# The end of the output projection: homes of the transposed parts, raw loads and the place of the last pair

## The chip, the cores and the metric

The kernel runs on one core of a Trainium2 chip. The metric is the device time of one execution in microseconds (us). The median of three runs of the kernel before is 1249.16 us (1244.13 to 1250.89).

PE is the matrix engine, DVE the vector engine, ACT the scalar engine, POOL the GpSimd engine, SP the engine that issues the DMAs. Each has its own queue of instructions and works through it in order; a semaphore holds the head of a queue back until what it needs is there.

## What is computed

One layer of an encoder block on 1024 tokens of width 1024, in float32:

```
u = RMSNorm(x);  [q|k|v|cB|cC|cH|gA|gB] = u @ W_in
A = neighbourhood attention(q, k, v, rpb);  B = cB * conv3(cC * cH)
m = sigmoid(gA) * (A @ W_A) + sigmoid(gB) * (B @ W_B)
x = x + m @ W_o
x = x + relu(RMSNorm(x) @ W1)^2 @ W2
```

The change lies where the product with `W_o` ends and the one with `W1` (1024 x 4096) begins.

## The kernel before

Every float32 operand of a matmul is split into two float16 parts, high and low, after scaling by a power of two, and each product takes three passes. The large products use a scheme with seven products in place of eight, so both operands are needed in seven forms (sums and differences of quarters).

**Order of the work.** The kernel is one long program, and what it issues on an engine is issued in the order in which its Python code runs. `unit` (L185) issues the matmuls of one unit and then calls `step()` and `tick()` some times. `step` advances all generators in the list `fg` by one `yield`; `tick` advances the first generator in `bg` that is not waiting. So the places of ACT's, DVE's and POOL's instructions among each other follow from the units at which the generators were advanced. `apart(mark, n, work)` lets a generator wait until `n` more matmul columns have been issued.

**Projection.** `proj(b, half)` computes one block of 128 tokens by 512 columns of `x + m @ W_o`; `tail(b, half, ...)` does so and then calls the given functions. The last eight blocks are the calls of `tail`, up to L1386. The actions are: `sq`, the sum of squares of a block for the norm (L1163); `begin` and `normal`, the scaling of a block into the form buffer `fv[0]` (L1173); `form_sums`, the additions that make seven forms of four quarters (L1155, DVE); `high(n, part)`, the float16 high part (L1189, ACT); `low(n, part)`, the low part (L1195, DVE) and the DMA that transposes both into `U2`, the moving operand of the next product (L1196, SP). Pairs `n` = 0 to 3 are 256 tokens each; part 0 are forms 0 to 3 (`u2T`), part 1 forms 4 to 6 (`u2x`). All pairs use the same float16 buffer `fv[1]`. `forms_m` makes the forms of weight group 1 (`mH` and others, L1293 to L1296); `g1` advances it. The last pair is done by `last_pair`, a generator in `fg` (L1391) that runs while PE is already in the next product.

**First MLP product.** `W1` is cut in 16 groups `q` of 256 columns. `quad(q)` issues seven units of 12 matmuls, in the order 1, 6, 5, 4, 2, 7, 3; what follows a unit is called its post:

| post | engine, line | |
|---|---|---|
| 1 | ACT L1453 | copy from PSUM |
| 6, 5 | DVE L1436, L1441 | need the copy |
| 2 | DVE L1455 | |
| 7 | DVE L1444, L1445, L1446 | three operations |
| 3 | DVE L1449 | then `h_done(q)` is put into `fg` |

`h_done(q)`: relu (L1410) and square (L1412) on ACT, four additions that make the forms of the next operand (`sums`, L1155), here on POOL, and the store to HBM (L1416). Quads 0 and 1 are done in two halves of 256 columns of the moving operand: the first halves of both, then the wait for pair 3, then the second halves. Their units take half as long, and the second halves go in the order 1, 2, 5, 4, 6, 7, 3.

**Weights of a group.** Each group has two raw pieces of 512 KB, loaded into five buffers `rawp` (L210). `load_upto` issues loads up to a count, less `held`, and not beyond `limit`. A group's preparation: `rows_scaled`, eight scalings of rows (L948, ACT); `forms_sum`, two sums of squares (L957, ACT) and four additions for the forms (L962, POOL); `sum_of`, a small reduction (L928) and a cast (L929) on DVE; `all_sum`, a matmul with ones that adds over the partitions (L179, PE), called the ones matmul below; the scale out of it (L182, L404 to L411, DVE); `forms_split`, four high parts (L977, ACT) and four low parts (L973, DVE). `sums1(q)` is the first half of this, `prep1(q)` the second, and `prep1(q)` goes on with `sums1(q + 1)`. Quad `q` needs group `q`; while quad `q` runs, the ones matmul of group `q + 2` and its split are issued.

The second MLP product follows at L1470 and below and is not touched.

Of the kernel before, what the change touches and what calls it, by code (L numbers as in the profile page):

```python
# [10 lines left out]
F32 = mybir.dt.float32  # L11
F16 = mybir.dt.float16
BF16 = mybir.dt.bfloat16
I32 = mybir.dt.int32
AF = mybir.ActivationFunctionType
OP = mybir.AluOpType
# [36 lines left out]
def encoder_block(ctx: ExitStack, tc: tile.TileContext, x, weights, cols, gqk, rel, masks, out):  # L53
    nc = tc.nc
    V, A, G, T, SP = nc.vector, nc.scalar, nc.gpsimd, nc.tensor, nc.sync

    base = ctx.enter_context(tc.tile_pool(name="base", bufs=1))
    rawp = ctx.enter_context(tc.tile_pool(name="rawp", bufs=5))
# [38 lines left out]
    def at(c, i, n=1):  # L97
        return slice(c.start + i, c.start + i + n)
# [18 lines left out]
    fg, bg = [], []  # L117
# [88 lines left out]
    loads, loaded, done, vhome, held, limit = [], [0], [0], [], [0], [10 ** 6]  # L206
# [5 lines left out]
    def load_upto(n):  # L212
        while loaded[0] < min(n - held[0], limit[0], len(loads)):
            ch, p = loads[loaded[0]]
            loaded[0] += 1
            t = rawp.tile([128, 1024], F32, name="raw")
            load_into(t[:, :ch.widths[p][0] * ch.widths[p][1]], ch, p)
            ch.raw.append(t)
# [103 lines left out]
    g1, g2, gm2 = at(consts, 0, 8), at(consts, 20, 8), keep()  # L322
    rows = {"A": lambda j: rowsA, "B": lambda j: rowsB, "O": lambda j: rowsM}
    chunks, offset = {}, 0
    for (kind, j), pieces in plan():
# [4 lines left out]
        for p, (k, w) in enumerate(ch.widths):  # L330
            ch.offs.append(offset)
            if kind != "X" and (kind, j) != ("1", 0) and (kind, j, p) != ("1", 1, 1):
# [3 lines left out]
    cV, cConv, cA, cB, cO, c1, c2, c2x = ([chunks[k, j] for j in range(n)] for k, n in  # L336
                                              (("V", 2), ("C", 4), ("A", 4), ("B", 4), ("O", 2),
                                               ("1", 16), ("2", 4), ("X", 4)))
# [120 lines left out]
    sq = w1p.tile([128, D], F32, name="sq", bufs=1)  # L459
# [84 lines left out]
    for p in range(11):  # L544
# [7 lines left out]
        for q in (p,) if p < 6 else (2 * p - 6, 2 * p - 5):  # L552
            c = q // 2 + 3
# [306 lines left out]
    for k in range(N + 11):  # L860
        p, w = k // 16, k % 16
# [212 lines left out]
    for n in range(8):  # L1074
# [19 lines left out]
        else:  # L1094
            push(cO[0])
            tick(4)
            y = w3p.tile([128, 4, 512], F32, name="gsum", bufs=1)
# [47 lines left out]
    U2 = (u2T,  # L1145
          w4p.tile([128, 3, 2, 4, 512], F16, name="u2x", bufs=1))
# [4 lines left out]
    def sums(f, sub):  # L1151

        z = [f[:, i] for i in range(7)]
        for o, a, b, op in ((5, 0, 2, OP.subtract), (2, 2, 3, OP.subtract), (4, 2, 0, OP.subtract), (6, 1, 4, OP.add)):
            sub.tensor_tensor(z[o], z[a], z[b], op=op)  # L1155
            yield

    pair_done, fv, ssq = [0], [], keep(10)
# [7 lines left out]
    def row_scale(col, n=1):  # L1166
        y = tmp(n)
        for _ in rstd(at(ssq, col, n), D, y, 9):
            pass
        return y  # L1170

    def normal(b, y):
        A.activation(fv[0][:, 2 * (b // 4):2 * (b // 4) + 2].rearrange("p a t -> p (a t)"), X1[:, b], AF.Copy,  # L1173
                     scale=sc[:, y])
# [9 lines left out]

    PART = ((0, 4), (4, 7))

    def high(n, part):
        a, b = PART[part]
        A.activation(fv[1][:, a:b, 0], fv[0][:, a:b], AF.Copy)  # L1189

    def low(n, part):

        f, v = fv
        a, b = PART[part]
        V.tensor_tensor(v[:, a:b, 1], f[:, a:b], v[:, a:b, 0], op=OP.subtract)  # L1195
        SP.dma_start_transpose(U2[a // 4][:, :, :, :, 128 * n:128 * n + 128]  # L1196
                               .rearrange("p f s k t -> p (f s k) t"), v[:, a:b].rearrange("p f s k -> p (f s k)"))
        pair_done[0] = n + part

    def form_sums():  # L1200
# [22 lines left out]
    def sums1(q):  # L1223

        ch = c1[q]
        if q == 2:
            yield from rows_scaled(ch, g2)
        if q == 0:
            tsum[0] = U2[1][:, 2].rearrange("p s k t -> p (s k t)").bitcast(F32).rearrange("p (i c) -> p i c", i=4)
        elif q % 2 == 0:  # L1230
            while q == 2 and pair_done[0] < 4:
                yield
            t = wsp.tile([128, 2, 4, 512], F32, name="tsum", tag="ws")
            for i in range(2):
                tsum[q + i] = t[:, i]
        if q != 2:
            yield from rows_scaled(ch, g2)
        yield from forms_sum(ch, tsum[q], 3 if q else 0)

    def prep1(q):  # L1240

        ch = c1[q]
        s, ch.inv = yield from scale_of(ch.sum, 9, 1)
        yield from gate(q)
        pool, tag = TAGS[q % 3]
        P = P1[q] = pool.tile([128, 7 if q else 8, 2, 512], F16, name="w16_1", tag=tag)
        yield from forms_split(ch, tsum[q], s, P)
        ready.add(q)
        if 1 < q < 15:
            yield from sums1(q + 1)  # L1250
# [1 line left out]
    SQJ = U2[1][:, 0, :, :, 384:512].rearrange("p s k t -> p (s k) t").bitcast(BF16)  # L1252
    scaled = []

    limit[0] = c1[3].first + 1

    def prep_m():

# [14 lines left out]
    def forms_m():  # L1273

        (w11, w12), (w21, w22) = ([c1[1].raw[i].rearrange("p (n m) -> p n m", n=2)[:, j] for j in range(2)]
                                  for i in range(2))
        s = scaled[0]
        two = rawp.tile([128, 1024], F32, name="raw").bitcast(F16).rearrange("p (f i c) -> p f i c", f=2, i=2)
        held[0], limit[0] = 1, 10 ** 6
        t2 = w4p.tile([128, 2, 512], F16, name="t2", bufs=1)  # L1280
        t4 = w4p.tile([128, 2, 512], F16, name="t4", bufs=1)
        k4 = lambda v: v.rearrange("p (k c) -> p k c", k=4)
        flat = {0: lambda i: P1[0][:, 7, i], 1: lambda i: two[:, 0, i], 2: lambda i: two[:, 1, i],
                5: lambda i: t2[:, i], 6: lambda i: t4[:, i]}

        def place(f, i):
            return k4(flat[f](i)) if f in flat else M[0][:, 4 * (f - 3):4 * (f - 3) + 4, 512 * i:512 * i + 128]

        P1[1] = lambda f, i, k: place(f, i)[:, k]
        src = {0: w11, 1: w21, 2: w22, 3: w11, 4: w12, 5: w22, 6: w21}  # L1290

        def hi(f):
            A.activation(place(f, 0), k4(src[f]), AF.Copy, scale=sc[:, s])  # L1293

        def lo(f):
            V.scalar_tensor_tensor(place(f, 1), k4(src[f]), sc[:, s], place(f, 0), op0=OP.mult, op1=OP.subtract)  # L1296

        def add(o, a, b):
            V.tensor_tensor(o, a, b, op=OP.add)

        hi(0), hi(2), hi(1), lo(0), add(w11, w11, w12), lo(2)
        yield
        add(w12, w12, w22)
        yield
        add(w22, w22, w11), lo(1), hi(5), add(w21, w21, w22), hi(6)
        yield
        lo(5), lo(6)
        yield
        hi(3), hi(4), lo(3)
        yield  # L1310
        lo(4)
        done[0] += 1
        load_upto(done[0] + 5)
        ready.add(1)

# [15 lines left out]
    def wait(n):  # L1331
        for _ in range(n):
            yield
# [7 lines left out]
    two = []  # L1341
# [9 lines left out]
    def tail(b, half, *acts):  # L1351
        proj(b, half, acts)
        for a in acts:
            a()
# [3 lines left out]
    def sq(b, half=None):  # L1358
        if half is None:
            return lambda: square(b, 2 * (b % 4) + b // 4)  # L1360
        return lambda: square(b, (6 if half == 0 else 8) + b // 4, slice(512 * half, 512 * half + 512))

    def row3(b):
        V.tensor_tensor(sc[:, at(ssq, 6 + b // 4)], sc[:, at(ssq, 6 + b // 4)], sc[:, at(ssq, 8 + b // 4)], op=OP.add)
        return row_scale(6 + b // 4)

    def do(f, *a):
        return lambda: f(*a)

    g1, tk = do(advance, chain), do(tick)  # L1370
# [6 lines left out]
    tail(5, 1, sq(1), form_sums, do(high, 0, 0), g1)  # L1377
    tail(2, 1, do(high, 0, 1), sq(5), do(low, 0, 0), do(begin, 1), do(low, 0, 1))
    tail(6, 1, sq(2), form_sums, do(high, 1, 0))
    tail(3, 0, sq(6), do(high, 1, 1), do(low, 1, 0), do(begin, 2), do(low, 1, 1))  # L1380
    tail(7, 0, sq(3, 0), form_sums, do(high, 2, 0), g1)
    bg.append(sums1(2))
    tail(3, 1, sq(7, 0), do(low, 2, 0), do(high, 2, 1), do(low, 2, 1), g1, tk)
    side[0] = False
    bg.extend(prep1(q) for q in range(2, 16))
    tail(7, 1, sq(3, 1), lambda: normal(3, row3(3)), tk)  # L1386
    fv[1] = wsp.tile([128, 7, 2, 512], F16, name="v16", tag="ws")

    def last_pair():
        sq(7, 1)()  # L1390
        y = row3(7)  # L1391
        yield from wait(3)
        normal(7, y)
        yield from wait(6)
        form_sums()
        high(3, 0), high(3, 1)
        yield from wait(6)
        low(3, 0), low(3, 1)

    fg.append(last_pair())  # L1400
    pe_done[0] = 0
# [6 lines left out]
    def h_done(q):  # L1408
        f = AS.pop(q)
        A.activation(f[:, 0:4], f[:, 0:4], AF.Relu)  # L1410
        yield
        A.activation(f[:, 0:4], f[:, 0:4], AF.Square, scale=sc[:, c1[q].inv],  # L1412
                     accum_out=sc[:, at(bsum[q // 4], q % 4)])
        yield
        yield from sums(f, G)
        SP.dma_start(HS[q // 4][:, :, q % 4], f)  # L1416
        live.remove(q)
        if q % 4 == 3:
            m = tmp()
            V.tensor_reduce(sc[:, m], sc[:, bsum[q // 4]], axis=AX, op=OP.max)  # L1420
            yield
            yield from pow2(m, 14, *R[q // 4])
            r_ready[q // 4] = True
# [293 lines left out]
```

## Time and profile before

| | |
|---|---|
| median of three runs | 1249.16 us |
| the profiled execution, its own time | 1249.31 us |
| its span in the trace | 1247.2 us, mean granted clock 0.992 |
| PE busy | 1203.7 us |
| DVE, ACT, POOL busy | 929.7, 765.1, 438.8 us |
| first unit of the first MLP product | 646.85 us from the span's start |
| first unit of the second MLP product | 951.04 us |

The span is counted from the first to the last instruction of the trace, and all starts below are from its start. A row of a timeline gives start, duration, engine, line, operation, output and input with their shapes, and the number of instructions; in brackets stands the idle time of the engine before it and what ended it. A matmul's row lasts until its result is written, so rows of consecutive units overlap by some 0.16 us. An `as` is the buffer of a quad's results, `v` the float16 buffer of the pairs, `form` the buffer `fv[0]`, `w` the split weights.

### The profile page before, as it was taken

The numbers are of one execution on the slowest core, as the hardware profiler recorded it, in microseconds if no ns is written. First come the engines' busy times: TensorE is split into PE (matmuls) and PEld (weight loads), VectorE is DVE, ScalarE is ACT, GpSimd is POOL, SyncE is SP. The second block draws the span as 40 slices with busy tenths as digits, with TensorE's granted clock in tenths as the row PEclk, the third lists the DMA queues.
The fourth block names the chain that finished last, engine by engine and source line by source line (L and its number), as shares of the span: only waits on it lengthen the run. The fifth ranks groups of instructions, "written<-read, shape, count | busy, mean of one in ns | idle before, by whom it ended". The sixth has DMA issues, their size and how long they took to land. (4 is left out here: it accounts for less than half of the span.)

```text
span 1247.2 us, 17068 instructions
## 1 busy us (share of the span) xinstructions
PE 1203.7 (97%) x6294; PEld 577.4 (46%) x6294; DVE 929.7 (75%) x1733; ACT 765.1 (61%) x1177; POOL 438.8 (35%) x297
## 2 busy tenths in 40 slices
PE   4989999998999999999998999999999999999998
PEld 3534444554444444444456444444444444444444
DVE  6668778878557686887867655554546999999997
ACT  5777567677464454536665867877855773645430
POOL 2340002221231111101002756556557463373562
PEclk8999999999999999999998999999999999999999
DMA  6458455656552211216185445544575743436202
GB/s 256 105 191 182 79 119 136 130 104 136 122 112 83 68 52 51 68 38 251 59 164 115 155 164 162 186 146 134 186 264 182 272 191 134 173 112 240 101 34 101
DMA packets 170803, 173.35 MB, mean 139 GB/s; under 512 B 131424, under 2 KB 131936, under 8 KB 166624
## 3 DMA queue, kind: packets, MB, share of 16 engines
q1 hardware_dynamic: 170720, 172.27, 46.9%
q8 instruction: 49, 0.80, 0.3%
q14 instruction: 34, 0.28, 0.1%
HBM read 102.51 MB, written 37.75 MB: 112 GB/s over the span
## 5 line engine op out<-in xcount | busy, mean ns | idle before, releaser
L188 PEld LDWEIGHTS <-ops 128*128 128x128 f16 x1356 | 132.4, 98 | 159.3 <-issue 2.4
L188 PEld LDWEIGHTS <-w 128*128 128x128 f16 x1368 | 133.1, 98 | 143.8 <-issue 5.2
L858 PE MATMUL ps_d<-uT,w_ws 128*128 128x512 f16 x528 | 126.5, 382 | 0.0
L188 PE MATMUL ps_d<-ops 128*128 128x512 f16 (+1 forms) x528 | 118.3, 374 | 0.0
L188 PE MATMUL ps_s<-ops 128*128 128x512 f16 x492 | 113.2, 379 | 1.5 <-DVE ops L1550 1.1
L1541 ACT ACTIVATE ops<-hf,sc 128x2048 f16<-128x2048 f32 x26 | 52.0, 1999 | 94.6 <-PE ps_o L188 35.1
L1155 POOL TENSOR_TENSOR as<-as 128x512 f32<-128x512 f32 x64 | 88.0, 1374 | 42.5 <-ACT as L1412 38.7
L188 PEld LDWEIGHTS <-uT 128*128 128x128 f16 x648 | 64.8, 101 | 70.8 <-issue 5.7
L962 POOL TENSOR_TENSOR tsum<-raw 128x512 f32<-128x512 f32 x28 | 47.4, 1709 | 137.0 <-ACT raw L948 137.0
L188 PEld LDWEIGHTS <-w_s 128*128 128x128 f16 x588 | 56.7, 98 | 69.4 <-DVE w_s L973 1.9
L188 PE MATMUL ps_d<-u2x,w 128*128 128x512 f16 (+1 forms) x360 | 80.0, 372 | 0.0
L1543 DVE SCALAR_TENSOR_TENSOR ops<-hf,sc,ops 128x2048 f16<-128x2048 f32 x26 | 73.8, 2838 | 5.2 <-ACT ops L1541 5.2
L188 PE MATMUL ps_o<-ops 128*128 128x512 f16 x336 | 77.1, 379 | 0.0
L858 PEld LDWEIGHTS <-w_ws 128*128 128x128 f16 x528 | 51.2, 98 | 53.5 <-issue 1.7
L188 PE MATMUL ps_o<-u2T,w 128*128 128x512 f16 (+1 forms) x324 | 73.2, 376 | 0.0
L948 ACT ACTIVATE raw<-raw,sc 128x256 f32<-128x256 f32 x172 | 71.1, 493 | 0.9 <-DMA raw<-in_weights 0.9
L962 POOL TENSOR_TENSOR gsum<-raw 128x512 f32<-128x512 f32 x14 | 19.0, 1374 | 131.5 <-issue 57.1
L1436 DVE TENSOR_TENSOR as<-ps_d,as 128x512 f32<-128x512 f32 (+1 forms) x15 | 10.1, 674 | 62.5 <-ACT as L1453 62.5
L977 ACT ACTIVATE w<-raw,sc 128x512 f16<-128x512 f32 (+1 forms) x28 | 24.6, 927 | 52.2 <-DVE sc L410 52.2
L805 ACT ACTIVATE sz<-sz,sc 128x384 f32<-128x384 f32 (+1 forms) x64 | 37.3, 583 | 27.6 <-DVE sc L796 16.2
L188 PE MATMUL ps_s<-u2T,w 128*128 128x512 f16 (+1 forms) x252 | 52.7, 359 | 0.0
L278 DVE SCALAR_TENSOR_TENSOR w_ws<-raw,sc,w_ws 128x512 f16<-128x512 f32 (+2 forms) x72 | 49.0, 733 | 3.7 <-ACT w_ws L290 3.7
(333 smaller groups left out, 2616.3 us busy)
## 6 DMA issues: line engine op xcount, KB each, us to landing
raw<-in_weights SPq DMA_DIRECT2D x89, 512.0 KB, 5.6
hs<-as SPq DMA_DIRECT2D x16, 1792.0 KB, 8.8
hf<-hs SPq DMA_DIRECT2D x26, 1024.0 KB, 6.7
w2x<-in_weights SPq DMA_DIRECT2D x16, 512.0 KB, 8.1
raw<-in_weights SPq DMA_DIRECT2D x16, 384.0 KB, 3.9
xt<-in_x SPq DMA_DIRECT2D x8, 512.0 KB, 10.2
gs<-s SPq DMA_DIRECT2D x4, 1024.0 KB, 6.7
x<-in_x SPq DMA_DIRECT2D x8, 512.0 KB, 9.7
```

The source lines that it names most:

```text
L188: T.matmul(ps, l, r, start=a, stop=b)
L278: V.scalar_tensor_tensor(lo, self.raw[p][:, o:o + m], sc[:, c:c + 1], hi, op0=OP.mult, op1=OP.subtract)
L805: A.activation(z, z, AF.Exp, scale=-1.0, bias=sc[:, d["mx"]], accum_out=sc[:, d["sm"]])
L858: T.matmul(ps, l, r, start=a, stop=b)
L948: A.activation(v, v, AF.Copy, scale=sc[:, at(g, 4 * i + k)])
L962: G.tensor_tensor(t[:, o], a, b, op=OP.add)
L977: A.activation(o(0), w, AF.Copy, scale=sc[:, s])
L1155: sub.tensor_tensor(z[o], z[a], z[b], op=op)
L1436: V.tensor_tensor(z[5], ps[6], z[4], op=OP.add)
L1541: A.activation(P[:, 1, 0], hf, AF.Copy, scale=sc[:, Rs])
L1543: V.scalar_tensor_tensor(P[:, 1, 1], hf, sc[:, Rs], P[:, 1, 0], op0=OP.mult, op1=OP.subtract)
```

## The change

- `high` and `low` of pair 1, part 0 write to two of the raw buffers (`spare`), in two pieces of two forms each with a transpose of their own; all others stay in `fv[1]`.
- `forms_m` takes three raw buffers in place of one. The loads are limited: of groups 2 and 3, three pieces were loaded early; now the first piece of group 2 alone. Its second piece is loaded when `forms_m` ends, both pieces of group 3 when `last_pair` ends.
- The actions of the last projection blocks are spread otherwise. The scaling of pair 2 is written out (`normal(2)`, `normal(6)` in place of `begin(2)`).
- `last_pair` issues its second low part three steps after the first.
- `sums1(2)` and the generators of groups 2 to 15 are put into `bg` at the end of `last_pair`, not during the last two projection blocks.
- The additions of `h_done` for quads 0 and 1 are on DVE in place of POOL.

```diff
--- before.py
+++ after.py
@@ -1184,17 +1184,25 @@
 
     PART = ((0, 4), (4, 7))
 
+    spare = []
+
+    def pieces(n, part):
+
+        a, b = PART[part]
+        if (n, part) != (1, 0):
+            return [(a, b, fv[1][:, a:b])]
+        return [(2 * i, 2 * i + 2, spare[i]) for i in range(2)]
+
     def high(n, part):
-        a, b = PART[part]
-        A.activation(fv[1][:, a:b, 0], fv[0][:, a:b], AF.Copy)
+        for a, b, v in pieces(n, part):
+            A.activation(v[:, :, 0], fv[0][:, a:b], AF.Copy)
 
     def low(n, part):
 
-        f, v = fv
-        a, b = PART[part]
-        V.tensor_tensor(v[:, a:b, 1], f[:, a:b], v[:, a:b, 0], op=OP.subtract)
-        SP.dma_start_transpose(U2[a // 4][:, :, :, :, 128 * n:128 * n + 128]
-                               .rearrange("p f s k t -> p (f s k) t"), v[:, a:b].rearrange("p f s k -> p (f s k)"))
+        for a, b, v in pieces(n, part):
+            V.tensor_tensor(v[:, :, 1], fv[0][:, a:b], v[:, :, 0], op=OP.subtract)
+            SP.dma_start_transpose(U2[a // 4][:, a % 4:a % 4 + b - a, :, :, 128 * n:128 * n + 128]
+                                   .rearrange("p f s k t -> p (f s k) t"), v.rearrange("p f s k -> p (f s k)"))
         pair_done[0] = n + part
 
     def form_sums():
@@ -1252,7 +1260,7 @@
     SQJ = U2[1][:, 0, :, :, 384:512].rearrange("p s k t -> p (s k) t").bitcast(BF16)
     scaled = []
 
-    limit[0] = c1[3].first + 1
+    limit[0] = c1[2].first
 
     def prep_m():
 
@@ -1275,8 +1283,12 @@
         (w11, w12), (w21, w22) = ([c1[1].raw[i].rearrange("p (n m) -> p n m", n=2)[:, j] for j in range(2)]
                                   for i in range(2))
         s = scaled[0]
-        two = rawp.tile([128, 1024], F32, name="raw").bitcast(F16).rearrange("p (f i c) -> p f i c", f=2, i=2)
-        held[0], limit[0] = 1, 10 ** 6
+        three = [rawp.tile([128, 1024], F32, name="raw").bitcast(F16).rearrange("p (f i c) -> p f i c", f=2, i=2)
+                 for _ in range(3)]
+        spare.extend(three[:2])
+        two = three[2]
+        held[0], limit[0] = 3, c1[2].first + 1
+        load_upto(done[0] + 5)
         t2 = w4p.tile([128, 2, 512], F16, name="t2", bufs=1)
         t4 = w4p.tile([128, 2, 512], F16, name="t4", bufs=1)
         k4 = lambda v: v.rearrange("p (k c) -> p k c", k=4)
@@ -1310,6 +1322,7 @@
         yield
         lo(4)
         done[0] += 1
+        held[0], limit[0] = 1, c1[3].first
         load_upto(done[0] + 5)
         ready.add(1)
 
@@ -1377,13 +1390,13 @@
     tail(5, 1, sq(1), form_sums, do(high, 0, 0), g1)
     tail(2, 1, do(high, 0, 1), sq(5), do(low, 0, 0), do(begin, 1), do(low, 0, 1))
     tail(6, 1, sq(2), form_sums, do(high, 1, 0))
-    tail(3, 0, sq(6), do(high, 1, 1), do(low, 1, 0), do(begin, 2), do(low, 1, 1))
-    tail(7, 0, sq(3, 0), form_sums, do(high, 2, 0), g1)
-    bg.append(sums1(2))
-    tail(3, 1, sq(7, 0), do(low, 2, 0), do(high, 2, 1), do(low, 2, 1), g1, tk)
+    y = []
+    tail(3, 0, sq(6), do(low, 1, 0), lambda: y.append(row_scale(4, 2)), do(high, 1, 1),
+         lambda: (normal(2, at(y[0], 0)), normal(6, at(y[0], 1))), do(low, 1, 1))
+    tail(7, 0, sq(3, 0), g1, form_sums, do(high, 2, 0))
+    tail(3, 1, sq(7, 0), do(low, 2, 0), g1)
     side[0] = False
-    bg.extend(prep1(q) for q in range(2, 16))
-    tail(7, 1, sq(3, 1), lambda: normal(3, row3(3)), tk)
+    tail(7, 1, sq(3, 1), do(high, 2, 1), do(low, 2, 1), lambda: normal(3, row3(3)))
     fv[1] = wsp.tile([128, 7, 2, 512], F16, name="v16", tag="ws")
 
     def last_pair():
@@ -1395,7 +1408,13 @@
         form_sums()
         high(3, 0), high(3, 1)
         yield from wait(6)
-        low(3, 0), low(3, 1)
+        low(3, 0)
+        yield from wait(3)
+        low(3, 1)
+        limit[0] = 10 ** 6
+        load_upto(done[0] + 5)
+        bg.append(sums1(2))
+        bg.extend(prep1(q) for q in range(2, 16))
 
     fg.append(last_pair())
     pe_done[0] = 0
@@ -1412,7 +1431,7 @@
         A.activation(f[:, 0:4], f[:, 0:4], AF.Square, scale=sc[:, c1[q].inv],
                      accum_out=sc[:, at(bsum[q // 4], q % 4)])
         yield
-        yield from sums(f, G)
+        yield from sums(f, G if q > 1 else V)
         SP.dma_start(HS[q // 4][:, :, q % 4], f)
         live.remove(q)
         if q % 4 == 3:
```

## The prediction

> **What bounds the kernel now.** I read the page first, then the waits of TensorE, the granted clock by stretches, and the timelines of the engines at the projection's end and in one steady stretch of the first MLP matmul.
>
> ```profile
> span 1247.2 us, 17068 instructions
> ...
> PE 1203.7 (97%) x6294; PEld 577.4 (46%) x6294; DVE 929.7 (75%) x1733; ACT 765.1 (61%) x1177; POOL 438.8 (35%) x297
> ...
> PEclk8999999999999999999998999999999999999999
> ```
>
> PE is busy for 97% of the span at nearly full clock, so little can be won: 1247.2 − 1203.7 = 43.5 us of idle in all, and what half clock costs. Between 600 and 960 us PE waits for other engines only here (times waited for, longest):
>
> ```profile
> PE ps_s L188 <- DVE as L1444: 6.1, 1, 6.1
> PE ps_s L179 <- DVE ones L929: 3.0, 1, 3.0
> PE ps_s L188 <- DVE as L1455: 0.5, 1, 0.5
> ```
>
> The change touches the places of the first two, and the loop behind them, which repeats for every weight group. One steady quad of before on PE, ACT, DVE and POOL (start, duration, instructions):
>
> ```profile
> 743.57 0.17 PE L179 MATMUL ps_s<-ones 128*128 128x1 bf16 x1
> ...
> 746.18 2.75 PE L188 MATMUL ps_d<-u2x,w 128*128 128x512 f16 x12
> ...
> 751.36 2.75 PE L188 MATMUL ps_o<-u2T,w 128*128 128x512 f16 x12
> ...
> 761.72 0.17 PE L179 MATMUL ps_s<-ones 128*128 128x1 bf16 x1
> ```
> ```profile
> 744.87 1.76 ACT L977 ACTIVATE w<-raw,sc 128x512 f16<-128x512 f32 x2 [4.61 <-DVE sc L410]
> ...
> 748.61 3.28 ACT L948 ACTIVATE raw<-raw,sc 128x256 f32<-128x256 f32 x8
> 751.80 1.04 ACT L957 ACTIVATE tsum<-raw 128x1024 f32<-128x1024 f32 x1
> ...
> 754.02 1.89 ACT L1410 ACTIVATE as<-as 128x2048 f32<-128x2048 f32 x1
> 755.95 2.00 ACT L1412 ACTIVATE as<-as,sc 128x2048 f32<-128x2048 f32 x1
> ...
> 757.95 0.57 ACT L1453 ACTIVATE as<-ps_o 128x512 f32<-128x512 f32 x1
> ```
> ```profile
> 746.99 1.94 DVE L973 SCALAR_TENSOR_TENSOR w<-raw,sc,w 128x512 f16<-128x512 f32 x2
> 748.85 2.47 DVE L973 SCALAR_TENSOR_TENSOR w<-tsum,sc,w 128x1024 f16<-128x1024 f32 x2
> 751.24 0.68 DVE L1444 TENSOR_TENSOR as<-ps_d,as 128x512 f32<-128x512 f32 x1
> ...
> 753.16 0.68 DVE L1449 TENSOR_TENSOR as<-ps_s,as 128x512 f32<-128x512 f32 x1
> 758.56 0.69 DVE L1436 TENSOR_TENSOR as<-ps_d,as 128x512 f32<-128x512 f32 x1 [4.71 <-ACT as L1453]
> ...
> 759.34 0.16 DVE L929 CAST ones<-sc 128x1 bf16<-128x1 f32 x1
> ```
> ```profile
> 754.26 2.62 POOL L962 TENSOR_TENSOR tsum<-tsum,raw 128x512 f32<-128x512 f32 x2 [0.56 <-ACT tsum L957]
> ```
>
> A quad's first unit starts at 751.36; units follow every (751.36 − 746.18)/2 = 2.59 us, and the ones matmul comes 761.72 − 743.57 = 18.15 us after the last one. It stands behind four units and needs the cast L929, which ended at 759.34 + 0.16 = 759.50: a slack of 2.2 us, no more. In queue order the cast hangs on post six (L1436), that on the copy of unit one (L1453), that on square and relu (L1412, L1410), and these on post three (L1449). ACT prepares the next group (L948, L957) in the 754.02 − 748.61 = 5.41 us before the relu, while post three was not there yet: that work is covered.
>
> **The change part by part.** I compared the order in which the two programs issue their instructions on each engine; line numbers are those of before.
>
> *Weight preparation in the loop.* The generators of groups 2 to 15 now start only after the last low part. They count PE columns, so they keep a phase for good, and it is now one PE unit later in the quad. Three things follow in quads 2 to 13, twelve times. (a) On ACT the order becomes relu, four L948, square, four L948, both L957, copy: the 5.41 us move from before the relu to behind it. (b) On DVE post seven (L1444 to L1446) stands ahead of the four L973, not behind them. (c) The ones matmul stands behind five units, and posts six and five both precede the cast.
>
> From the quad start at 751.36 with these rows: unit seven ends at 746.18 + 2.75 = 748.93; post seven takes 753.16 − 751.24 = 1.92, to 750.9; the L973 take 751.24 − 746.99 = 4.25, to 755.1; post three 0.68, to 755.8 (before: 753.84). From relu to the end of the copy ACT now needs 5.41 + (757.95 − 754.02) + 0.57 = 9.91, to 765.8. Post six and the cast take 759.50 − 758.52 = 0.98, post five 1.92/3 = 0.64 more, to 767.4. PE reaches the ones matmul at 751.36 + 5 × 2.59 = 764.3. So it stalls 3.1 us where it had 2.2 to spare. The stall does not die out: behind it come unit seven, post seven, L973 and so on, and from ones to ones it is 2.75 + 1.92 + 4.25 + 0.68 + 9.91 + 1.6 and some 0.1 of handing over = 21.2 us, against 18.15: +3.1 for each quad at full clock. POOL's two last additions follow L957 and are 2.6 us later wanted only by the third L977, some 3 us behind the ones matmul: hidden; without that cover they would be 2.62 more.
>
> What a stall does to the clock is shown by the 3.03 us that before has at the same matmul (in the second view: stretch, length, PE busy, granted clock):
>
> ```profile
> 705.83 0.16 PE L179 MATMUL ps_s<-ones 128*128 128x1 bf16 x1 [3.03 <-DVE ones L929]
> 705.86 4.18 PE L188 MATMUL ps_o<-u2T,w 128*128 128x512 f16 x12
> ```
> ```profile
> 705.36:708.77 3.41, 2.94 (x8) 0.50 0.05 17
> ```
>
> The clock was half for 3.41 us, and the unit behind the stall took 4.18 instead of 2.75: +1.43. Behind the new stall that unit is unit seven, which is in the loop. So a quad costs +3.1 to +4.5. Not each stall will lie like this one; I take +4.3, nearer the row.
>
> By the Trainium skill ("TensorE: Matmul & The Clock Gate", Part 1: The HAM clock gate) the clock falls to half after at least one idle window of about 3.4 us; a stall of 3.1 us would then leave it whole, and each quad would cost 3.1. The trace speaks against it: 3.03 us were enough.
>
> *The last low part behind post seven, and what stood before it.*
>
> ```profile
> 647.20 1.78 DVE L1296 SCALAR_TENSOR_TENSOR mH<-raw,sc,mH 128x512 f16<-128x512 f32 x1
> ...
> 658.42 2.87 DVE L1155 TENSOR_TENSOR form<-form 128x512 f32<-128x512 f32 x4 [0.24 <-ACT form L1173]
> ...
> 661.87 3.96 DVE L1195 TENSOR_TENSOR v<-form,v 128x2048 f16<-128x2048 f32 x2 [0.25 <-ACT v L1189]
> ```
> ```profile
> 652.95 1.69 ACT L948 ACTIVATE raw<-raw,sc 128x256 f32<-128x256 f32 x4
> ```
> ```profile
> 666.22 2.72 PE L188 MATMUL ps_s<-u2T,t 128*128 128x256 f16 x12 [6.13 <-DVE as L1444]
> ...
> 673.91 1.47 PE L188 MATMUL ps_d<-u2T,w 128*128 128x256 f16 x12
> ```
> ```profile
> 591.21 2.98 SPq L210 DMA_DIRECT2D raw<-in_weights  x3
> ...
> 664.19 4.81 SPq L1196 DMA_TRANSPOSE u2T<-v  x1
> 669.10 4.30 SPq L1196 DMA_TRANSPOSE u2x<-v  x1
> ```
> ```profile
> u2T<-v SPq DMA_TRANSPOSE x4, 7.1
> ```
>
> PE's 6.13 us wait is for post seven of quad 0's first half, which stood on DVE behind both low parts of pair 3. Now the second one (three of seven forms, 3.96 × 3/7 = 1.7) stands behind it; and a piece of mH (1.78 on DVE) and four L948 (1.69 on ACT) no longer stand ahead of pair 3. That is 1.7 + 3 us sooner, and the wait falls below 2.5. But quad 0's second half needs the transpose of pair 3's first part: issued some 3 us sooner, at 661, and landed 7.1 later (the median of the four) to 9.7 (what passed between 664.19 and the unit that reads it): 668 to 671 instead of 673.91. Gain 3 to 6; I take 5, nearer the median.
>
> *The spare homes* release the first high part of pair 1 from the transpose of pair 0. No wait of PE hangs on it in the waits above: nothing. The additional transpose is one more issue on SP, idle between the pairs. If ACT were late there, it would be part of the 3 us.
>
> *The late raws.* Group 2's second load goes out behind a transpose of pair 2 and is read 10 us later: nothing. Both loads of group 3, which lay there since 591, now stand on SP behind both transposes of pair 3: 661 + 4.8 + 4.3 = 670, landed around 675. On ACT the L948 and L957 of group 3 (5.41), then relu and square of quad 0 (3.93), come to about 684; quad 0's sums, now on DVE, put two or three additions of 2.87/4 = 0.7 in front of the cast: 686.5. PE comes to that ones matmul twelve half units (2.59/2 each) after 669, at 684.5. A stall of 2 (0 to 3.5), with up to 1.4 for the clock: I take 3, which gives back most of the 5.
>
> *Sums of quad 1 on DVE:* two of the additions stand before the cast of quad 2: +1.5, once. Quad 0's are in the 3.
>
> **Sum.** Quads 2 to 13: 12 × 4.3 = +51.6. Quad 2 of before had its own 3.03 + 1.43, now counted twice: −4.5. Quad 0: −5. Late raws and quad 0's sums: +3. Quad 1's sums: +1.5. Together +46.6. On the profiled execution (1249.31 us by its own time, 2.1 of it around the span; the median of the runs is 1249.16, so one base serves) that is 1296. Behind quad 13 no group is left to prepare, PE is bound as before, and the delay stays to the end.
>
> **The rivals.**
> A, a stall costs only itself: 3.1 us of idle leaves the clock at full. 12 × 3.1 = 37.2, less the same 5 for the rest: 1282. Against it: half clock behind 3.03 us. For it: one stall only shows it. The rule of the Trainium skill above would give this time.
> B, the loop is longer than these rows. In quad 2 of before POOL's sums ran beside the L973, and the pair that reads the sums took longer than the 2.47 above:
>
> ```profile
> 712.54 3.49 DVE L973 SCALAR_TENSOR_TENSOR w<-tsum,sc,w 128x1024 f16<-128x1024 f32 x2
> ```
>
> One us more in each quad is +12: 1308. Against: by the order POOL's sums end before the L973 begin.
> C, faster: the moved 5.41 us stay covered, as relu and copy come early enough. The loop must lose 3.1 of its 21.2; that holds from the point where the four L973 (4.25) are through before post seven. Then the 5 of quad 0 and the 4.5 of quad 2 are won, and the late raws cost 3 or nothing: 1243 or 1240. Against: DVE's order puts post seven first, and the queues of this trace run in order.
> D, the change does nothing that counts: SP's transposes land pair 3 no sooner, and the loop has its slack: 1249. Against: ACT's order is plainly another.
>
> **How the numbers follow.** Forecast 0.62, with a range of its own of 12 × 3.7 to 12 × 4.7, less 5: 1289 to 1301. A 0.14; B 0.11; C 0.08; D 0.05. The range takes in A with 5 us less (the late raws and quad 1's sums hidden) and B with 4 more: 1277 to 1312. About 0.5% (6.2 us) is what a measurement can tell here from no change. Forecast, A and B are slower by more: 0.87. Of C, at −6 to −9, 0.05 is faster; the rest of it and D are the same: 0.08.
>
> **What would show it.** The wait for post seven under 2.5 us; quad 0's second half starting near 669; a wait of PE for the cast of about 2 us before quad 2; then twelve more for the cast, 3 to 4 us each, 21 to 23 us apart, with half clock behind most; on ACT the relu directly behind the L977 with idle before it, and the copy last. If the quads still come every 18.15 us, the prediction is wrong at its root; if every 21.2, rival A holds.

## The result, and the profile after

| | before | changed |
|---|---|---|
| median of the runs beside each other | 1250.03 us | 1303.72 us (1302.46 to 1304.98) |
| ratio, 95% interval | | 1.0441 (1.0419 to 1.0463) |
| span of the profiled execution | 1247.2 us | 1302.5 us |
| granted clock, mean | 0.992 | 0.982 |

The changed kernel is 4.4% slower; 55.3 us stand between the two spans. The page of the changed kernel, busy time by engine and the chain that ended last (in this region a line of the changed kernel has a number 19 higher than in the kernel before: L1410 is L1429, L1449 is L1468, L1453 is L1472; so L1455 is here post six, and L1474 is post two):

```profile
PE 1218.8 (94%) x6294; PEld 580.8 (45%) x6294; DVE 932.2 (72%) x1742; ACT 764.9 (59%) x1178; POOL 419.2 (32%) x289
...
PE 26%; ACT 11%; DVE 10%; issue 3%; DMA 1%; DVEq 0%; ACTq 0%
```

ACT and DVE have hardly more work than before, yet 11% of the chain that ended last is ACT's (3% before). PE is busy 15.1 us longer with the same 6294 matmuls: that is time at a lower granted clock. The rest is idle time of PE, and its waits between 600 and 1020 us say where:

```profile
PE ps_o L179 <- DVE ones L929: 34.4, 10, 6.1
PE ps_o L179 <- DVE sc L108: 10.0, 3, 3.9
PE ps_s L188 <- DVE as L1463: 3.9, 1, 3.9
PE ps_s L188 <- DVE as L1474: 2.4, 1, 2.4
PE ps_o L188 <- DMA u2T<-v: 0.5, 1, 0.5
```

Thirteen waits of the ones matmul in place of one: 44.4 us. (Three are put down to L108, a small operation that DVE issues right behind the cast; the cast is what is waited for in each.) One steady loop on PE, ACT and DVE:

```profile
779.91 0.16 PE L179 MATMUL ps_o<-ones 128*128 128x1 bf16 x1 [3.74 <-DVE ones L929]
802.91 0.16 PE L179 MATMUL ps_o<-ones 128*128 128x1 bf16 x1 [3.01 <-DVE ones L929]
802.94 4.29 PE L188 MATMUL ps_d<-u2x,w 128*128 128x512 f16 x12
```
```profile
791.30 1.91 ACT L1429 ACTIVATE as<-as 128x2048 f32<-128x2048 f32 x1 [6.16 <-DVE as L1468]
793.12 1.69 ACT L948 ACTIVATE raw<-raw,sc 128x256 f32<-128x256 f32 x4
794.71 1.99 ACT L1431 ACTIVATE as<-as,sc 128x2048 f32<-128x2048 f32 x1
...
796.70 1.69 ACT L948 ACTIVATE raw<-raw,sc 128x256 f32<-128x256 f32 x4
798.29 1.04 ACT L957 ACTIVATE tsum<-raw 128x1024 f32<-128x1024 f32 x1
...
800.51 0.58 ACT L1472 ACTIVATE as<-ps_o 128x512 f32<-128x512 f32 x1
```
```profile
784.40 0.69 DVE L1463 TENSOR_TENSOR as<-ps_d,as 128x512 f32<-128x512 f32 x1 [3.08 <-PE ps_d L188]
...
786.34 1.94 DVE L973 SCALAR_TENSOR_TENSOR w<-raw,sc,w 128x512 f16<-128x512 f32 x2
788.19 2.47 DVE L973 SCALAR_TENSOR_TENSOR w<-tsum,sc,w 128x1024 f16<-128x1024 f32 x2
790.58 0.68 DVE L1468 TENSOR_TENSOR as<-ps_s,as 128x512 f32<-128x512 f32 x1
801.12 0.69 DVE L1455 TENSOR_TENSOR as<-ps_d,as 128x512 f32<-128x512 f32 x1 [9.86 <-ACT as L1472]
```

ACT stands idle for 6.16 us ahead of the relu, with the raws of the next group ready, and then does all of the next group's preparation while everything else waits: DVE 9.86 us for the copy, PE 3.01 us for the cast. The work that used to fill ACT's idle time now stands behind what ACT waits for.

### The profile page after: what moved, and what is told of

The parts are those of the page before. It is cut to its first block, busy times and chain, and to the rows that moved or that the text cites. A ratio compares the mean times of both kernels' runs of the same rounds, so it can differ in the third digit from the quotient of the medians.

```text
span 1302.5 us, 17091 instructions
## 1 busy us (share of the span) xinstructions
PE 1218.8 (94%) x6294; PEld 580.8 (45%) x6294; DVE 932.2 (72%) x1742; ACT 764.9 (59%) x1178; POOL 419.2 (32%) x289
## 4 chain that ended last, share of the span: by engine, by line
PE 26%; ACT 11%; DVE 10%; issue 3%; DMA 1%; DVEq 0%; ACTq 0%
PE ps_d L188 12%; PE ps_s L188 8%; PE ps_o L188 6%; DVE w L973 4%; ACT raw L948 3%; ACT as L1429 2%; ACT as L1431 2%; ACT tsum L957 1%; DVE ops L1569 1%; DVE as L1460 1%; DVE as L1455 1%; DVE as L1463 1%; DVE as L1468 1%; DVE as L1465 1%; DMA u2T<-v 1%
## 5 line engine op out<-in xcount | busy, mean ns | idle before, releaser
L188 PEld LDWEIGHTS <-w 128*128 128x128 f16 x1368 | 136.1, 100 | 194.2 <-issue 63.2
L962 POOL TENSOR_TENSOR tsum<-raw 128x512 f32<-128x512 f32 x28 | 36.8, 1315 | 238.3 <-ACT raw L948 238.3
L1455 DVE TENSOR_TENSOR as<-ps_d,as 128x512 f32<-128x512 f32 (+1 forms) x15 | 10.1, 674 | 123.4 <-ACT as L1472 123.4
L188 PE MATMUL ps_d<-u2x,w 128*128 128x512 f16 (+1 forms) x360 | 93.0, 415 | 0.0
L188 PE MATMUL ps_s<-u2T,w 128*128 128x512 f16 (+1 forms) x396 | 85.7, 366 | 0.0
L1155 POOL TENSOR_TENSOR as<-as 128x512 f32<-128x512 f32 x56 | 76.8, 1371 | 20.1 <-ACT as L1431 16.8
L1429 ACT ACTIVATE as<-as 128x2048 f32<-128x2048 f32 x16 | 30.6, 1909 | 80.8 <-DVE as L1468 80.8
L948 ACT ACTIVATE raw<-raw,sc 128x256 f32<-128x256 f32 x172 | 72.0, 493 | 0.8 <-DMA raw<-in_weights 0.8
L179 PE MATMUL ps_o<-ones 128*128 128x1 bf16 x24 | 4.0, 165 | 57.5 <-DVE ones L929 34.4
L977 ACT ACTIVATE w<-raw,sc 128x512 f16<-128x512 f32 (+1 forms) x28 | 24.7, 927 | 48.1 <-DVE sc L410 48.1
```

The source lines that it names most:

```text
L188: T.matmul(ps, l, r, start=a, stop=b)
L948: A.activation(v, v, AF.Copy, scale=sc[:, at(g, 4 * i + k)])
L962: G.tensor_tensor(t[:, o], a, b, op=OP.add)
L977: A.activation(o(0), w, AF.Copy, scale=sc[:, s])
```

## The experiments

Twelve kernels. The first four ask which edit brought the order about; the next four whether that order is the loss, and which part of it; three more what is left when it is mended, and the last one whether the sums on DVE have a part in it. Each ratio is to runs of the kernel before taken beside it. Edits in the code shift the line numbers of a kernel by a line or two.

**Three steps between the low parts, alone, in the kernel before.**

```diff
-        low(3, 0), low(3, 1)
+        low(3, 0)
+        yield from wait(3)
+        low(3, 1)
```


> The kernel before with one edit: three steps between the two low parts of the last pair. Theory (these three steps put the weight generators one unit later, through group 2's forms, which wait for the last low part; relu then stands ahead of the weight preparation on ACT): quads 2 to 13 come every 22.6 us instead of 18.15, total 1250 + 11 x 4.5 + about 1 = 1295 to 1303. Rival 1 (the late start of the generators sets the phase, as the prediction put it) and rival 2 (the late raws of group 3 set it): neither is in this kernel, so 1244 to 1251.

Measured: 1300.95 us, ratio 1.0424 (1.0403 to 1.0446). PE's waits for the cast number thirteen again:

```profile
PE ps_o L179 <- DVE ones L929: 30.5, 10, 4.4
PE ps_o L179 <- DVE sc L108: 10.8, 3, 3.9
```

So one edit, without homes, late raws, sums on DVE or a late start, brings nearly the whole loss.

**The generators' start where it was, in the changed kernel.**

```diff
+    bg.append(sums1(2))
-    tail(3, 1, sq(7, 0), do(low, 2, 0), g1)
+    tail(3, 1, sq(7, 0), do(low, 2, 0), g1, tk)
     side[0] = False
+    bg.extend(prep1(q) for q in range(2, 16))
...
         load_upto(done[0] + 5)
-        bg.append(sums1(2))
-        bg.extend(prep1(q) for q in range(2, 16))
```


> The changed kernel with sums1(2) and the generators of groups 2 to 15 put into bg where the kernel before has it, during the last projection blocks; all else as changed. Theory (the three steps set the phase): as the changed kernel, 1300 to 1305, quads every 22.6 us. Rival 1 (the late start of the generators): quads every 18.15 us, 1246 to 1252.

Measured: 1305.85 us, ratio 1.0459 (1.0437 to 1.0481), just above the expected range. No help.

**The late start alone, in the kernel before** (the two lines moved to the end of `last_pair`).

> The kernel before with sums1(2) and the generators of groups 2 to 15 put into bg at the end of last_pair; all else as before. Theory (three steps): quads every 18.15 us, 1245 to 1252; four to eight L948 fewer before pair 3, so perhaps 1 to 2 us less. Rival 1 (late start): quads every 22.6 us, 1295 to 1305.

Measured: 1248.49 us, ratio 0.9992 (0.9980 to 1.0005): nothing, neither the loss nor the 1 to 2 us less. With the run before it, the late start is out as a cause.

**The low parts together again, in the changed kernel** (the first diff, undone).

> The changed kernel without the three steps: both low parts of the last pair together again, ahead of post seven. Theory (three steps): quads every 18.15 us, 1247 to 1253, the 6 us wait for post seven partly back. Rival 2 (late raws of group 3, loaded at the end of last_pair, set the phase or cost it): 1300 or more.

Measured: 1251.86 us, ratio 1.0024 (1.0012 to 1.0035). The loop is back at 18.15 us:

```profile
783.03 0.17 PE L179 MATMUL ps_s<-ones 128*128 128x1 bf16 x1
801.18 0.17 PE L179 MATMUL ps_s<-ones 128*128 128x1 bf16 x1
```

and the wait for post seven is 5.9 us again. With the first run this settles it: the three steps, and they alone. The way is read from the code: `sums1(2)` waits `while q == 2 and pair_done[0] < 4`, and `pair_done` becomes 4 in the last `low`. That wait was there before; three steps are one unit of a half quad; what group 2 loses there, every later group keeps.

**One constant, once, in the changed kernel.**

```diff
-        yield from forms_sum(ch, tsum[q], 3 if q else 0)
+        yield from forms_sum(ch, tsum[q], (2 if q == 5 else 3) if q else 0)
```


> The changed kernel with one constant changed for one group: the sum of group 5 comes two units of columns after its forms, not three. Theory (the loop is a matter of phase alone): from quad 4 on, ACT has the weight preparation ahead of the relu again and quads come every 18.15 us; ten quads of 4.5 us less: 1254 to 1262. Rival (contention, buffers or loads make the quads slow): still 22.6 us, 1300 or more.

Measured: 1260.44 us, ratio 1.0108 (1.0088 to 1.0127). The ones matmuls of its trace:

```profile
710.95 0.16 PE L179 MATMUL ps_o<-ones 128*128 128x1 bf16 x1 [4.44 <-DVE ones L929]
733.05 0.16 PE L179 MATMUL ps_s<-ones 128*128 128x1 bf16 x1 [4.80 <-DVE ones L929]
754.83 0.16 PE L179 MATMUL ps_s<-ones 128*128 128x1 bf16 x1 [1.01 <-DVE ones L929]
772.98 0.17 PE L179 MATMUL ps_s<-ones 128*128 128x1 bf16 x1
791.14 0.17 PE L179 MATMUL ps_s<-ones 128*128 128x1 bf16 x1
```

Two long waits, one short one, and then none: 18.15 us from there on. The same buffers, loads and instructions run without a stall once the phase is moved one unit.

**Relu two steps later, in the changed kernel.**

```diff
         f = AS.pop(q)
+        yield
+        yield
         A.activation(f[:, 0:4], f[:, 0:4], AF.Relu)
```


> The changed kernel with the relu of h_done two steps later, so that on ACT the copy of the next quad's unit one comes ahead of relu and square; the ones matmul and post seven stay where the change has put them. Theory (the 9.9 us chain relu, weights, copy, cast is what PE waits for): the chain is cut at the relu, quads come every 18.15 us, 1242 to 1250. Rival (post seven ahead of the L973 on DVE, or five units ahead of the ones matmul, is what costs): 22 us or more per quad, 1290 to 1304.

Measured: 1266.65 us, ratio 1.0152 (1.0130 to 1.0175). The total missed the range, but the loop did as the theory said: from 728.73 to 892.12 ten ones matmuls come without a wait, 18.15 us apart.

```profile
728.73 0.17 PE L179 MATMUL ps_o<-ones 128*128 128x1 bf16 x1
746.88 0.17 PE L179 MATMUL ps_o<-ones 128*128 128x1 bf16 x1
...
892.12 0.17 PE L179 MATMUL ps_o<-ones 128*128 128x1 bf16 x1
```

In this kernel post seven still stands ahead of the four L973 and the ones matmul behind five units. So of the three things that the order changed, (b) and (c) cost nothing by themselves; the loss needs (a), ACT's preparation between the relu and the copy. Whether (a) would cost as much without (b) was not tried: by the prediction's rows (b) puts post three, and so the relu, some 2 us later. What the total lost is at the other end: at 892.12 this kernel is 0.7 us behind the kernel before at the same place (888.81 + 2.62), at the end 19.4 us (spans of 1266.6 and 1247.2). ACT's waits of this kernel between 700 and 960 us show a new one,

```profile
ACT as L1474 <- DMA hs<-as: 37.5, 11, 11.9
```

the copy of a quad waits for the store of the quad two before, whose buffer it takes over and which now leaves later. In the steady loop it is hidden. A wait of 5.78 us for the cast (at 943.06) is new as well, and the waits at the start of the second product are longer (up to 3.19 us, where the kernel before has at most 0.76); whether they come of the late stores was not tried.

**The same edit in the kernel before.**

> The kernel before with the same edit: relu two steps later, behind the copy. Theory: the 3.03 us wait of quad 2 and its 1.4 us of half clock go, the rest stays: 1244 to 1247. Rival (the wait of quad 2 comes of late weights, not of the relu ahead of the copy): 1249 to 1251.

Measured: 1284.95 us, ratio 1.0302 (1.0284 to 1.0320): a plain miss. Both theories had left the store out.

```profile
ACT as L1455 <- DMA hs<-as: 82.0, 12, 12.6
```
```profile
764.28 0.16 PE L179 MATMUL ps_s<-ones 128*128 128x1 bf16 x1 [1.61 <-DVE ones L929]
784.83 0.16 PE L179 MATMUL ps_s<-ones 128*128 128x1 bf16 x1 [2.24 <-DVE ones L929]
```

Here the ones matmul has one unit less of cover, the copy waits for the store in every quad, and quads come 18.4 to 20.9 us apart (20.55 between the two rows). So the order relu, square, copy has its use: it lets the store go early.

**Three steps less ahead of the first low part, in the changed kernel** (`wait(3)` for `wait(6)`, so that the second low part stands where it stood before).

> The changed kernel with three steps in place of six ahead of the first low part of the last pair, so that the second stands where the kernel before has it and the phase of the weights is as before. Theory: quads every 18.15 us, and the gain of the projection's end stays, less the late raws of group 3: 1243 to 1250. Rival (the change's other parts cost): 1255 or more.

Measured: 1251.58 us, ratio 1.0032 (1.0019 to 1.0044). The loop is mended, but this kernel's wait for post seven is 6.4 us: both low parts are ahead of it again. The expected gain at the projection's end is not there, and the total lies just above the expected range.

**The phase mended at group 2, the change otherwise complete** (the constant above, with `q == 2`).

> The changed kernel, complete, with the phase mended at the first group: the sum of group 2 comes two units of columns after its forms, not three. Theory (phase is the whole loss): no wait for the cast from quad 3 on, 1246 to 1252; what is left against the kernel before is the sum of a shorter wait for post seven, the late raws and the sums on DVE. Rival (homes, raws or sums cost something in every quad): 1257 or more.

Measured: 1249.51 us, ratio 1.0015 (1.0001 to 1.0028). So all that the change does besides the phase comes to about nothing. Its waits show two that trade against each other: 4.4 for post seven (6.1 before), and 3.8 and 2.4 around quad 2 (3.0 before).

**Three edits in the kernel before:** the three steps, the late start and the constant at group 2; without homes, late raws and sums on DVE.

> The kernel before with three edits: the three steps between the low parts, the generators put into bg at the end of last_pair, and two units for the sum of group 2. It has neither the spare homes nor the late raws nor the sums on DVE. Theory: the phase of before, and post seven 1 to 2 us sooner: 1243 to 1249. Rival (post seven's place is worth nothing, as pair 3's transposes set the end): 1248 to 1250.

Measured: 1244.53 us, ratio 0.9969 (0.9957 to 0.9981), the fastest kernel of this study, 0.3% ahead of the kernel before, with the whole interval below 1. Its waits of PE between 600 and 1020 us:

```profile
PE ps_s L188 <- DVE as L1446: 3.6, 1, 3.6
PE ps_s L188 <- DVE as L1447: 1.7, 1, 1.7
PE ps_s L188 <- DVE ops L1552: 1.1, 2, 0.8
PE ps_s L179 <- DVE ones L929: 0.9, 1, 0.9
...
```

Post seven (L1446 here) costs 3.6 us instead of 6.1, and the 3.0 us ahead of quad 2's ones matmul have become 1.7 and 0.9; behind neither did the clock fall (1.00 from 699.0 to 706.8, and units of 2.75 us).

**The phase mended, sums on POOL, the loads' limit lifted earlier, in the changed kernel.**

```diff
-        held[0], limit[0] = 1, c1[3].first
+        held[0], limit[0] = 1, 10 ** 6
...
-        yield from sums(f, G if q > 1 else V)
+        yield from sums(f, G)
```


> The changed kernel with the phase mended at group 2, the sums of quads 0 and 1 on POOL again, and no limit on loads from the end of forms_m, so that group 3's first piece comes earlier. Theory (late raws and sums on DVE make the waits for the cast in quads 1 and 2): 3 to 5 us less than the same kernel without the last two edits, 1243 to 1248. Rival (those waits are the loop's start and come back as in the kernel before): the same as that kernel.

Measured: 1247.80 us, ratio 0.9994 (0.9981 to 1.0007), against 1249.51 without these two edits: 1.7 us in the medians, less than the 3 to 5 expected, though the two waits around quad 2 did shrink to 1.7 and 0.9. A wait that none of the other kernels has at this length took some of it back:

```profile
PE ps_s L188 <- ACT as L1472: 1.6, 1, 1.6
```

Three loads now go out at 647.02, ahead of the transpose of pair 2 (648.64), and ACT's copy of quad 0 stands idle for 6.34 us until that transpose has landed. The homes that stay in it are no gain over the kernel without them.

**Sums on POOL, in the changed kernel.**

> The changed kernel with the sums of quads 0 and 1 on POOL, as before. Theory: the loop keeps its 22.6 us, the wait of quad 2 shrinks by the 1.5 us of two additions, that of quad 1 too: 1299 to 1303. Rival 3 (the sums on DVE set the loop back): 1250 to 1290.

Measured: 1299.08 us, ratio 1.0417 (1.0386 to 1.0448). That is 4.6 us less than the changed kernel in the medians, which were not taken beside each other; the intervals of the ratios overlap. The waits are clearer: that of quad 2 is 4.40 us in place of 6.10, that of quad 1 0.80 in place of 2.46, and the loop is as slow. The sums are a cost of quads 1 and 2, not of the loop.

## Why the prediction was right, point by point

The forecast was 1296 with 1277 to 1312 as its range; the time is 1303.7. The mechanism was that of the forecast in the loop, which makes most of the loss; its terms at both ends were further off, all on the same side. The terms, and what the two traces show (from PE's starts):

| term | predicted | measured | from |
|---|---|---|---|
| up to the start of quad 2 | −2 (−5 and +3) | +0.3 | 692.28 before, 692.56 after |
| quad 2, up to the place of the changed ones matmul | +1.3 | +1.6 | 709.87 before, 711.78 after |
| eleven loops | 11 × 4.3 = 47.3 | 249.06 − 199.71 = 49.4 | ones matmuls 711.78 to 960.84; before, the same places, 709.87 to 906.96 + 2.62 |
| behind quad 13 | 0 | +4.0 | the rest of 55.3 |

**The loop.** Its working held: 9.91 us from relu to the copy's end were predicted, 801.09 − 791.30 = 9.79 came; 4.25 for the L973, 790.58 − 786.34 = 4.24 came. The stall was put at 3.1 us; the eleven behind quad 2 are 2.65 to 3.86, with a mean of 3.25. The mean loop is 249.06/11 = 22.64 us, +4.5 per quad, the upper end of the bounds where 4.3 was taken. The granted clock, in the stretch of some 3.4 us behind three of the waits:

```profile
779.91:783.30 3.39, 3.39 (x10) 0.53 0.00 0
...
802.91:806.30 3.39, 3.38 (x12) 0.66 0.00 0
825.78:829.20 3.42, 3.42 (x17) 1.00 0.00 0
```

So not every stall costs clock, as said; but a loop without it was still 22.06 us long (757.85 to 779.91), not 21.2, for two reasons of 0.7 and 0.1: the first two L973 then ran beside POOL's sums and took 2.67 us in place of 1.94 (rival B's mechanism, in a few quads), and posts six and five with the cast take 1.75 rather than 1.62. Rival A fell with the lower clock, which followed eight of the twelve stalls; C and D fell with the first wait.

**The cause of the phase** was named wrongly. The prediction put it to the generators' starting only after the last low part. The late start alone does nothing (1248.49), the early start does not help (1305.85); the three steps alone do it (1300.95). The order of the two programs, on which the numbers rest, was right; the reason that the prediction gave for it was read off the diff, and `sums1(2)`'s wait for the last pair was left out of it. The forecast survived since it used the order, not the reason.

**Three things under one price.** The prediction reckoned (a), (b) and (c) together. The run with the later relu shows that (b) and (c) alone cost nothing; (a) without (b) has no run.

**Quad 0** was predicted to gain 5 us; its second half began at 671.54 instead of 673.91: 2.4. The step that failed is that ACT and DVE come to pair 3 some 3 us sooner. They came 0.6 sooner, for a wait that the prediction did not name:

```profile
656.37 0.38 ACT L1472 ACTIVATE as<-ps_s 128x256 f32<-128x256 f32 x1 [4.14 <-DMA u2x<-v]
656.65 1.14 ACT L1173 ACTIVATE form<-x,sc 128x1024 f32<-128x1024 f32 x1
```

The copy of quad 0's unit one writes into the buffer that pair 2's float16 parts leave, so it waits for their transpose to land (issued at 649.59), and the scaling of pair 3 stands behind it on ACT. What was saved ahead of it became idle time. Before, the same copy ended at 656.69. The late start alone in the kernel before shows the same: with the L948 ahead of pair 3 gone, the copy waits 2.81 us for that transpose, and the scaling starts at 656.34, 0.9 sooner than before. The wait for post seven fell to 3.9 us, not under 2.5, for the same reason.

**Late raws and quad 0's sums:** a wait of 2.46 us for the cast ahead of quad 2, as predicted (2, with 3 for it and the clock), but not for the raws. The prediction lets ACT start on group 3 when its loads have landed, at 675. ACT starts at 677.79 without a wait, directly behind the L977 of group 2, so the trace shows no cost of the late loads. (Nor had both lain there since 591 in the kernel before: the second went out at 654.43.) With the sums on POOL the wait is 0.80, so 1.7 of it are the sums; the rest is the place of the cast, which now stands behind the copy and so behind relu and square. That the term came out is in part luck. **Quad 1's sums** were put at 1.5 and two additions; they took 2.50 us, beside POOL's additions, where two just before them took 1.42, and the wait of quad 2 was 6.10, with a unit of 4.43 behind it.

**Behind quad 13** nothing was predicted. The wait for post two at the second product's start is 2.45 us where it was 0.5, and the clock fell behind it (0.68 of full, units of 4.12 and 3.11): 2.0 and 1.7. The low clock behind the last ones matmul is 1.7 (a unit of 4.44), and two waits of the kernel before, 1.1 together, are gone; that makes 4.3, near the 4.0. Why DVE is later there was not pursued.

## What to carry to other kernels

Where work is placed by counting steps, a wait moved by one unit at the start of a pipeline can shift everything behind it for good: compare the order of the instructions in the steady loop, far behind the edit, not only around it. In an engine's queue, put work that is ready ahead of the instruction that waits; the same instructions on the other side of it cost 5.4 us of cover here, and, with the lower clock, 4.5 us in each of eleven loops. A slack that the profile shows as no wait at all (2.2 us) is worth knowing before anything is moved.

## What the runs showed of the hardware

Idle times of the same length were followed by a lower granted clock in one quad and not in another: behind 3.01 us (802.91) it was 0.66 of full over the next 3.4 us, behind 2.86 us (825.78) and 3.06 us (757.85) it stayed at 1.00. Behind all four waits of 3.7 to 3.9 us it fell (0.52 to 0.63), and each of those follows a loop that had kept its full clock: PE reaches the ones matmul sooner there, and waits longer. So a stall of some 3 us costs between nothing and 1.7 us beyond itself (a unit of 4.43 instead of 2.75), and the eleven loops differ by 1 us (22.05 to 23.07) though their instructions are the same but for a few small ones of DVE in every fourth.
